# A batched matmul with scale and add: the mid-kernel transfers cut to four tiles, in another order

## The chip, the cores and the metric

The kernel runs on one core of a Trainium2 chip. The metric is the device time of one execution in microseconds. Lower is better.

## The reference

```python
batch, m, k, n = 16, 512, 1024, 768       # all float32
def reference(x, weight, scale, add_value):
    return (scale * np.matmul(x, weight) + add_value).astype(np.float32)
```

The batch and row dimensions flatten to 8192 rows of x (33.6 MB). The weight is 1024 x 768 (3.1 MB), the added tensor and the output are 8192 x 768 (25.2 MB each). Everything together, 87 MB moves between HBM and the chip's working memory.

## The kernel before

The 8192 rows are cut into 64 tiles of 128 rows. The row that a tile puts on partition p is row 64p + t, so several consecutive tiles of one partition lie side by side in HBM, and one transfer can fetch n tiles as 128 rows of n x 4 KB (x) or n x 3 KB (the added tensor and the output).

Two large buffers hold the tiles in rotation: `xs` has 24 slots for x (tile t in slot t modulo 24), `ao` has 24 slots for the added tensor. The result of a tile is written over its slot of `ao`, and the output is stored from there. So a load of the added tensor for tile t can only be issued when the store of tile t - 24 has landed, and a load of x for tile t only when tile t - 24 has been cast.

The work on one tile goes like this.
- Most tiles: GpSimd casts x to bf16 (`cast_to`, L129), TensorE transposes it (L139), ScalarE copies the transposed tile out of the accumulator memory (L145), TensorE multiplies it with the weight in 16 matmuls (`product`, L161), and VectorE scales the sum and adds the `ao` slot (`finish`, L169).
- Nine pairs of tiles (`PAIRS`: 14 and 15, 19 and 20, up to 54 and 55): GpSimd casts both into `vx` (`cast_pair`, L102), VectorE turns them in 32 x 32 blocks into `vt` (`turn_pair`, L113), in four parts over four steps. TensorE doesn't transpose these.
- The first three tiles are handled apart in `head`, interleaved with the arrival of the weight, which is cast on VectorE (L97).

`step` issues one tile: half of its matmuls, then the transposes of the next tile, the cast of the tile after it and, where a pair lies seven tiles ahead, that pair's casts; then the other half, the sum, and a part of a pair's turn. GpSimd executes its casts in this order, so a pair's casts stand ahead of later tiles' casts.

All transfers are issued by the one engine SyncE (SP), on one queue, in the order of the list `STREAM`. Its entries are (kind, first tile, number of tiles): x, weight (w), added tensor (a), output (o), and the left and right part of the last tile's output (l, r). An entry's kind says what SP must wait for: a store waits for the sums of its tiles, a load for free slots. SP works its list in order, so an entry that waits holds up those behind it. The compiled program also uses eight semaphores for transfers in turn, so that the issue of a transfer waits for the landing of the eighth one before it.

The order of the other engines' instructions follows from the same loop over `STREAM`: entries that need results run as many steps as they require.

Of the kernel before, what the change touches and what calls it, by code (L numbers as in the profile page):

```python
# [11 lines left out]
STREAM = [  # L12
    ("x", 0, 1), ("x", 1, 1), ("x", 2, 1), ("w", 0, 1), ("w", 1, 1), ("w", 2, 1),
    ("w", 3, 1), ("w", 4, 1), ("w", 5, 1), ("x", 3, 1), ("w", 6, 1), ("w", 7, 1),
    ("a", 0, 3), ("x", 4, 4), ("a", 3, 1), ("a", 4, 4), ("x", 8, 4), ("x", 12, 4),
    ("a", 8, 8), ("x", 16, 8), ("a", 16, 8), ("x", 24, 8), ("o", 0, 8), ("o", 8, 8),
    ("a", 24, 4), ("x", 32, 4), ("a", 28, 8), ("a", 36, 4), ("x", 36, 8), ("o", 16, 8),
    ("x", 44, 4), ("a", 40, 8), ("x", 48, 4), ("o", 24, 8), ("x", 52, 8), ("a", 48, 4),
    ("o", 32, 8), ("a", 52, 4), ("a", 56, 8), ("x", 60, 4), ("o", 40, 8), ("o", 48, 8),
    ("o", 56, 4), ("o", 60, 2), ("o", 62, 1), ("l", 63, 1), ("r", 63, 1),  # L20
]

X_SLOTS = 24
# [267 lines left out]
```

## Time and profile before

| | us |
|---|---|
| median of 11 runs | 213.59 (211.66 to 215.73) |
| the profiled execution's own time | 213.94 |
| its span, first to last instruction | 212.0 |
| TensorE matmul busy | 194.1 |
| VectorE busy | 131.0 |
| GpSimd busy | 63.5 |
| ScalarE busy | 49.4 |
| transfer queue, share of 16 engines' span | 97.9% |

All numbers below that come from the profile are of that one execution. The profile names engines PE (TensorE), DVE (VectorE), ACT (ScalarE), POOL (GpSimd) and SP (SyncE); "SPq" is SP's own queue of transfer issues. A group or a wait is given by line, engine and operation, written tile and read tile. The forty slices divide the span into stretches of 5.3 us; a digit is the busy share in tenths.

### The profile page before, as it was taken

The numbers are of one execution on the slowest core, as the hardware profiler recorded it, in microseconds if no ns is written. First come the engines' busy times: TensorE is split into PE (matmuls) and PEld (weight loads), VectorE is DVE, ScalarE is ACT, GpSimd is POOL, SyncE is SP. The second block draws the span as 40 slices with busy tenths as digits, with TensorE's granted clock in tenths as the row PEclk, the third lists the DMA queues.
The fourth block names the chain that finished last, engine by engine and source line by source line (L and its number), as shares of the span: only waits on it lengthen the run. The fifth ranks groups of instructions, "written<-read, shape, count | busy, mean of one in ns | idle before, by whom it ended". The sixth has DMA issues, their size and how long they took to land.

```text
span 212.0 us, 3009 instructions
## 1 busy us (share of the span) xinstructions
PE 194.1 (92%) x1195; PEld 118.4 (56%) x1218; DVE 131.0 (62%) x223; ACT 49.4 (23%) x52; POOL 63.5 (30%) x69
## 2 busy tenths in 40 slices
PE   7776399999999999999999899999999999999960
PEld 3443256656666556565656556565656666666630
DVE  1448122319999569859499498986980995322330
ACT  3603123233112113022031031121130310333210
POOL 1310523550080180710900714508007510133000
PEclk9999889999999999999999999999999999999996
DMA  6999999999999999999999999999999999999994
GB/s 239 409 417 444 405 439 414 442 445 420 439 427 456 414 427 422 379 441 433 443 424 428 436 414 439 413 420 425 447 395 429 422 383 413 351 420 434 420 410 176
DMA packets 6781, 87.22 MB, mean 411 GB/s; under 512 B 752, under 2 KB 880, under 8 KB 2928
## 3 DMA queue, kind: packets, MB, share of 16 engines
q1 hardware_dynamic: 6768, 87.03, 97.9%
q8 instruction: 9, 0.15, 0.3%
q14 instruction: 4, 0.03, 0.0%
HBM read 61.87 MB, written 25.17 MB: 410 GB/s over the span
## 4 chain that ended last, share of the span: by engine, by line
DMA 44%; PE 39%; DVE 5%; POOL 4%; issue 3%; SPq 1%; ACT 0%; POOLq 0%; ACTq 0%
DMA xs<-in_x_dram 41%; PE mm L161 35%; PE tp L139 4%; DVE vt L113 3%; DMA ao<-in_weight_dram 3%; POOL xb L129 2%; POOL vx L102 2%; DVE ao L169 2%; SPq L241 1%; ACT xt L145 0%; SPq L93 0%; POOLq L129 0%; POOLq L102 0%; ACTq L145 0%
## 5 line engine op out<-in xcount | busy, mean ns | idle before, releaser
L161 PE MATMUL mm<-w_bf,xt 128*128 128x256 bf16 (+1 forms) x719 | 127.9, 327 | 2.8 <-DVE w_bf L97 1.3
L161 PEld LDWEIGHTS <-xt 128*128 128x128 bf16 x736 | 69.0, 98 | 51.7 <-ACT xt L145 10.8
L169 DVE SCALAR_TENSOR_TENSOR ao<-mm,ao 128x768 f32<-128x768 f32 (+2 forms) x62 | 58.3, 944 | 56.4 <-PE mm L161 42.9
L145 ACT COPY xt<-tp 128x1024 bf16<-128x1024 bf16 (+1 forms) x49 | 46.7, 960 | 150.1 <-PE tp L139 150.1
L113 DVE STREAM_TRANSPOSE vt<-vx 32x256 f32<-32x256 f32 x144 | 62.7, 436 | 6.9 <-POOL vx L102 4.7
L129 POOL CAST xb<-xs 128x1024 bf16<-128x1024 f32 x43 | 43.4, 1040 | 42.7 <-DMA xs<-in_x_dram 30.0
L161 PE MATMUL mm<-w_bf,vt 128*128 128x256 bf16 (+1 forms) x282 | 49.1, 325 | 0.3
L102 POOL CAST vx<-xs 128x1024 bf16<-128x1024 f32 x18 | 18.2, 1040 | 81.7 <-DVE vt L113 44.3
L161 PEld LDWEIGHTS <-vt 128*128 128x128 bf16 x288 | 28.0, 98 | 17.8 <-DVE vt L113 0.3
L139 PE MATMUL tp<-identity,xb 128*128 128x128 f32 x184 | 28.8, 278 | 6.8 <-POOL xb L129 5.7
L139 PEld LDWEIGHTS tp<-identity,xb 128*128 128x128 f32 x184 | 21.5, 142 | 13.8 <-POOL xb L129 6.8
L97 DVE CAST w_bf<-ao 128x768 bf16<-128x768 f32 x8 | 4.5, 560 | 4.8 <-DMA ao<-in_weight_dram 4.8
L87 PE MATMUL warm<-zeros 128*128 128x512 bf16 x10 | 3.7, 546 | 1.2 <-DVE zeros L75 1.2
L125 DVE CAST xb<-xs 128x512 bf16<-128x512 f32 x3 | 1.3, 427 | 4.7 <-DMA xs<-in_x_dram 4.7
L127 POOL CAST xb<-xs 128x512 bf16<-128x512 f32 x2 | 1.7, 866 | 4.6 <-DMA xs<-in_x_dram 4.6
L87 PEld LDWEIGHTS <-zeros 128*128 128x128 bf16 x10 | 1.2, 133 | 3.2 <-issue 1.9
L228 DVE TENSOR_TENSOR ao<-ao 128x768 f32<-128x768 f32 x3 | 2.7, 951 | 0.0
L197 DVE TENSOR_SCALAR ao<-mm 128x768 f32<-128x768 f32 x2 | 1.8, 953 | 1.0 <-PE mm L161 1.0
L127 ACT ACT_TABLE_LOAD x1 | 1.3, 1283 | 0.7 <-PEq L272 0.7
L127 ACT CAST xb<-xs 128x512 bf16<-128x512 f32 x1 | 0.6, 618 | 2.2 <-DMA xs<-in_x_dram 2.2
L194 ACT ACTIVATE ao<-mm 128x768 f32<-128x768 f32 x1 | 0.8, 817 | 0.0
L75 DVE MEMSET zeros<- 128x256 uint32 x1 | 0.3, 272 | 0.9 <-PEq L272 0.9
(6 smaller groups left out, 0.9 us busy)
## 6 DMA issues: line engine op xcount, KB each, us to landing
out_dram<-ao SPq DMA_DIRECT2D x7, 3072.0 KB, 23.9
xs<-in_x_dram SPq DMA_DIRECT2D x4, 4096.0 KB, 33.9
ao<-in_add_value_dram SPq DMA_DIRECT2D x5, 3072.0 KB, 16.1
xs<-in_x_dram SPq DMA_DIRECT2D x7, 2048.0 KB, 17.0
ao<-in_add_value_dram SPq DMA_DIRECT2D x5, 1536.0 KB, 16.5
ao<-in_weight_dram SPq DMA_DIRECT2D x8, 384.0 KB, 7.3
xs<-in_x_dram SPq DMA_DIRECT2D x4, 512.0 KB, 4.6
out_dram<-ao SPq DMA_DIRECT2D x1, 1536.0 KB, 13.1
```

What stands on the lines that cost most here:

```text
L87: nc.tensor.matmul(warm[:, 0:CUT], zeros[:, 0:P], zeros, start=True, stop=True)
L97: nc.vector.tensor_copy(w_bf[:, j + i, :], ao[:, s + i, :])
L102: nc.gpsimd.tensor_copy(vx[:, i, :], xs[:, (t0 + i) % X_SLOTS, :])
L113: nc.vector.transpose(vt[b:b + 32, :, 32 * a:32 * a + 32], pairs[32 * a:32 * a + 32, :, b:b + 32])
L127: other(xb[:, K // 2:K], src[:, K // 2:K])
L129: nc.gpsimd.tensor_copy(xb, src)
L139: nc.tensor.transpose(tp[:, c, :], pairs[:, c * P:(c + 1) * P], identity)
L145: nc.scalar.copy(dst[:, c:c + q, :, :], src[:, c:c + q, :, :])
L161: nc.tensor.matmul(mm_tiles[t, cols[0]][:, n0:n1], lhs(t, j), w_bf[:, j, n0:n1], start=(j == 0), stop=(j == KJ - 1))
L169: nc.vector.scalar_tensor_tensor(a, mm_tiles[t, part][:, n0:n1], float(scale), a, op0=mybir.AluOpType.mult, op1=mybir.AluOpType.add)
L228: nc.vector.tensor_add(ao[:, t, :], ao[:, EARLY_AT + t, :], ao[:, t, :])
L241: nc.sync.dma_start(xs[:, k:k + n, :], x_v[:, s:s + n, :])
```

## The change

The list `STREAM` is replaced. The first twelve entries (four tiles of x and the weight, one tile each) and the last four (two tiles, one tile and two parts of one) stay. In between, every transfer is now four tiles long, apart from the first four tiles of the added tensor, which are loaded as three and one as they were. Before, 16 of the transfers in between were eight tiles long: seven stores, five loads of the added tensor and four loads of x. The list has 63 entries where it had 47. The order differs too: the first store stands behind 20 tiles of x and 12 of the added tensor, where it stood behind 32 and 24. The load of x for tiles 4 to 7 stands behind the load of the added tensor for tile 3, where it stood ahead of it.

```diff
 STREAM = [
     ("x", 0, 1), ("x", 1, 1), ("x", 2, 1), ("w", 0, 1), ("w", 1, 1), ("w", 2, 1),
     ("w", 3, 1), ("w", 4, 1), ("w", 5, 1), ("x", 3, 1), ("w", 6, 1), ("w", 7, 1),
-    ("a", 0, 3), ("x", 4, 4), ("a", 3, 1), ("a", 4, 4), ("x", 8, 4), ("x", 12, 4),
-    ("a", 8, 8), ("x", 16, 8), ("a", 16, 8), ("x", 24, 8), ("o", 0, 8), ("o", 8, 8),
-    ("a", 24, 4), ("x", 32, 4), ("a", 28, 8), ("a", 36, 4), ("x", 36, 8), ("o", 16, 8),
-    ("x", 44, 4), ("a", 40, 8), ("x", 48, 4), ("o", 24, 8), ("x", 52, 8), ("a", 48, 4),
-    ("o", 32, 8), ("a", 52, 4), ("a", 56, 8), ("x", 60, 4), ("o", 40, 8), ("o", 48, 8),
-    ("o", 56, 4), ("o", 60, 2), ("o", 62, 1), ("l", 63, 1), ("r", 63, 1),
+    ("a", 0, 3), ("a", 3, 1), ("x", 4, 4), ("a", 4, 4), ("x", 8, 4), ("a", 8, 4),
+    ("x", 12, 4), ("x", 16, 4), ("o", 0, 4), ("x", 20, 4), ("a", 12, 4), ("x", 24, 4),
+    ("a", 16, 4), ("a", 20, 4), ("o", 4, 4), ("a", 24, 4), ("a", 28, 4), ("x", 28, 4),
+    ("o", 8, 4), ("x", 32, 4), ("a", 32, 4), ("o", 12, 4), ("x", 36, 4), ("x", 40, 4),
+    ("o", 16, 4), ("x", 44, 4), ("a", 36, 4), ("x", 48, 4), ("o", 20, 4), ("a", 40, 4),
+    ("o", 24, 4), ("o", 28, 4), ("a", 44, 4), ("o", 32, 4), ("a", 48, 4), ("x", 52, 4),
+    ("o", 36, 4), ("o", 40, 4), ("a", 52, 4), ("x", 56, 4), ("x", 60, 4), ("a", 56, 4),
+    ("o", 44, 4), ("o", 48, 4), ("a", 60, 4), ("o", 52, 4), ("o", 56, 4), ("o", 60, 2),
+    ("o", 62, 1), ("l", 63, 1), ("r", 63, 1),
 ]
```

The code is otherwise the same, three lines further down.

## The prediction

> **What bounds the kernel now.** I read the totals by engine and the forty slices first, then what SP's issues waited for, then the rate by stretch, and last the chain and the timelines around those places where the matmul waits.
>
> ```profile
> PE 194.1 (92%) x1195; PEld 118.4 (56%) x1218; DVE 131.0 (62%) x223; ACT 49.4 (23%) x52; POOL 63.5 (30%) x69
> PEclk9999889999999999999999999999999999999996
> DMA  6999999999999999999999999999999999999994
> GB/s 239 409 417 444 405 439 414 442 445 420 439 427 456 414 427 422 379 441 433 443 424 428 436 414 439 413 420 425 447 395 429 422 383 413 351 420 434 420 410 176
> q1 hardware_dynamic: 6768, 87.03, 97.9%
> ```
>
> Two resources are full at once: TensorE 92% of the span, the transfer queue 97.9%. The traffic is fixed: 87.03 MB whatever the order. After 5 us no slice of the DMA row is below 9 until the last, so the only ways to change the end are the rate, an empty queue, or a matmul that finishes so late that the last stores find no backlog.
>
> ```profile
> core 0: us, PE busy (x) PEld busy (x) DVE busy (x) ACT busy (x) POOL busy (x), PEclk, DMA share, GB/s
> 5.30:13.00 7.70, 6.46 (x37) 3.68 (x38) 4.06 (x8) 3.22 (x6) 1.73 (x2) 1.00 1.03 409
> 25.00:37.00 12.00, 11.90 (x69) 7.46 (x71) 2.87 (x3) 3.83 (x4) 4.66 (x5) 0.88 1.01 429
> 41.50:71.00 29.50, 29.29 (x188) 18.30 (x191) 23.10 (x42) 8.10 (x8) 8.92 (x9) 1.00 1.00 430
> 80.00:170.00 90.00, 88.36 (x556) 54.49 (x566) 70.70 (x128) 19.23 (x19) 31.95 (x32) 1.00 1.00 425
> 170.00:187.00 17.00, 16.89 (x108) 10.42 (x108) 9.71 (x15) 4.05 (x4) 2.08 (x2) 1.00 0.98 382
> ```
>
> The windows' last column is the rate. Single tiles (3 and 4 KB a row) reach 409 GB/s; four-tile loads at 25 to 37 us 429; eight-tile loads at 41.5 to 71 us 430. So four tiles as such are nearly as fast as eight. Once stores share the queue it is 425, and at 170 to 187 us only 382; another window, 80 to 205 us, answers 419.
>
> ```profile
> SPq L247 <- DMA out_dram<-ao: 97.8, 5, 33.8
> SPq L255 <- DVE ao L169: 60.5, 8, 18.8
> out_dram<-ao SPq DMA_DIRECT2D x7, 3072.0 KB, 23.9
> xs<-in_x_dram SPq DMA_DIRECT2D x4, 4096.0 KB, 33.9
> ao<-in_add_value_dram SPq DMA_DIRECT2D x5, 3072.0 KB, 16.1
> ```
>
> SP waits 97.8 us for a store to free ao slots before an add load (L247), but the queue has tens of us of work by then, so this costs nothing while enough lies ahead of the waiting issue. The x7, x4 and x5 are the sixteen eight-tile transfers.
>
> ```profile
> 39.42 2.02 POOL L102 CAST vx<-xs 128x1024 bf16<-128x1024 f32 x2 [2.77 <-DMA xs<-in_x_dram]
> 41.39 3.01 POOL L129 CAST xb<-xs 128x1024 bf16<-128x1024 f32 x3
> 160.28 2.02 POOL L102 CAST vx<-xs 128x1024 bf16<-128x1024 f32 x2 [11.58 <-DMA xs<-in_x_dram]
> 44.73 0.60 PE L139 MATMUL tp<-identity,xb 128*128 128x128 f32 x4
> 121.05 0.66 PE L139 MATMUL tp<-identity,xb 128*128 128x128 f32 x4 [0.90 <-POOL xb L129]
> 164.64 0.60 PE L139 MATMUL tp<-identity,xb 128*128 128x128 f32 x4
> ```
>
> GpSimd runs in order: a pair's two casts (L102) whose x is late hold up the ordinary casts (L129) that TensorE's next transposes need. TensorE has one such gap in 180 us, 0.90 us at 121. Its end is 205.2 us; the last store is issued at about 205.6, its landing and the closing waits fill the rest of the 212.0 us span. In the trace's landing records the sixteen parts of the last transfer land from 208.6 to 211.15: one DMA engine is some 2.6 us behind the others, and it sets the end. Its backlog hides a later matmul.
>
> **What the Trainium skill says.** DMA: Bandwidth & Descriptors, Bandwidth, gives 78% of peak for a lone 1 MB transfer and 97% for 16 MB. Here the trace disagrees in size, because transfers queue back to back: 1.5 to 2 MB give 429 GB/s. Its part on small descriptors names a fixed overhead per packet; the trace agrees: in the packet records a 12,288 B row takes 460 ns (median), a 24,576 B row 912, a 16,384 B row 611, a 32,768 B row 1213, so 8 ns more for two halves of the add or output rows and 9 ns for x. Its part on the anatomy of one DMA says that waits happen on the issuing sequencer; SP's waits above agree, so a blocked issue holds up all later ones. Its part on completion says that sixteen engines finish independently and only all of them count as landed; the 2.6 us spread is that.
>
> **The change, part by part.** Only SP's list changes; PE, DVE, ACT and POOL instructions keep their kinds, counts and order.
>
> (1) Sixteen more transfers, 47 to 63. Each DMA engine takes 8 of the 128 rows and one 9 ns completion write. Twelve splits of add or output: 12 x (8 x 8 + 9) = 876 ns. Four of x: 4 x (8 x 9 + 9) = 324 ns. Sum 1.20 us on a full queue, nothing beside it: I count it whole. Sixteen more issues on SP (0.33 to 0.43 us each, near 6 us) are free: SP is waiting anyway.
>
> (2) Stores begin earlier and alternate more. Before the first store lie 29.36 MB now and 18.35 MB afterwards, so it moves at about 44 instead of 71 us (11.0 MB at 430). The changes between reads and writes go from 9 to 21. At the mixed rate of 419 against 430 for 27 us: 2.6% of 27 = 0.7 us. Bounds: 0 if alternation isn't what slows it; if the loss scales with the changes, 125 us x 2.6% = 3.2 us becomes 7.5, so +4.3. I take 0.7: in the 80 to 170 us window four of these changes pass at 425.
>
> (3) Waits on ao slots. Before, the add load of tile 56 waits for the store of 32 to 39, with one four-tile load ahead of it (issued at 171.30); that is where 382 GB/s stands. It goes. New is the add load of tile 28, which needs the store of tiles 4 to 7 landed with only the add load of 24 between: 3.7 us of queue against the spread of up to 2 us plus some 2 us from issue to first byte. The faster engines may stand empty for 0 to 0.6 us near 78 us; the slow one, still behind, doesn't. Also at most eight transfers can be unfinished (eight semaphores in turn; the ninth issue waits for the first): eight of 1.6 to 2.1 MB are still 30 us of work, so this costs nothing. I count 0.
>
> (4) TensorE. x of tiles 4 to 7 now goes behind the add load of tile 3: 24.47 - 23.50 = 0.97 us later, and TensorE is waiting for just that (4.8 us idle at 24.7), so all later steps move by 0.97. The x of 12 to 15 goes behind a further add load, 39.37 + 3.7 = 43.1; two pair casts and one plain (3.0) give 46.1 against a transpose wanted at 44.73 + 0.97 = 45.7: with the handover 0.5 us. The x of 52 to 55 has 67.11 MB up to its end, before 66.06: 160.1 + 2.5 + some 0.7 of part 1 + 0.5 of part 2 = 163.8, casts to 167.0, against 164.64 + 0.97 + 0.5 - 0.9 = 165.2: 1.8 us. The 0.90 at 121 goes, as x of 36 to 39 comes 7 us earlier. TensorE ends at 205.2 + 0.97 + 0.5 + 1.8 - 0.9 = 207.6, the last issue at 208.0. The first load, on an empty queue, needs 3.4 us with 1.3 of moving; the last store moves 0.4, so 2.5: 210.5. The queue's end is 211.15 + 1.2 + 0.7 = 213.05, so TensorE's 2.4 us stay hidden, with 2.5 us to spare.
>
> Sum: 213.94 (the profiled execution's own time, 1.9 above its span) + 1.20 + 0.7 = 215.8. That execution lies 0.35 above the median of 213.59 and I make no allowance for it, the eleven runs being spread from 211.66 to 215.73.
>
> **Rivals.**
> - *Only the row overhead* (no loss from mixing): 213.94 + 0 to 1.2, some 215.0. For it: 425 in the 80 to 170 us window. Against: slices of 379, 395, 383, 351, all after stores began.
> - *TensorE or the alternation becomes the bound.* Adds are late too: that of 60 to 63 has 82.31 of 87.03 MB up to its end, which the queue now reaches half-way between landings at 196.6 and 203.8, so 200.2 + 1.9 = 202.1; its first sum is wanted at 196.4 + 2.4 = 198.8. That of 56 to 59 lands where x of 60 does now, 188.8 + 1.9 = 190.7, against 184.1 + 2.4 = 186.5. Three accumulators let TensorE run two tiles (6 us) ahead, so this is covered by 2 us. If mixing costs 3 us rather than 0.7, x of 52 slips 2 us more, the adds 2 to 3, and TensorE ends near 210.5: 213.94 + 1.2 + 3 = 218.1. Against: it needs a rate of 410, seen in single stretches only.
> - *Not slower.* The weak stretch at 170 to 187 us costs (430 - 382)/430 x 17 = 1.9 us, and stems from the one narrow wait of part 3. The new order issues all loads after 150 us well ahead, so if the stretch returns to 430 and nothing replaces it: 213.94 + 1.2 - 1.9 = 213.2. It decides if the gain exceeds 1.2. Against: the same stretch holds slow packets of x of 60, whose issue was not late; and tile 28 has a narrow wait of its own.
>
> **How the numbers follow.** Forecast (215.8, within 1 us) 0.50; overhead alone 0.22; worse 0.16; not slower 0.12. About 1% is what a measurement of this kernel can tell from no change, here 211.5 to 215.7. The forecast lies on that line: 0.33 slower, 0.17 same. With the worse case 0.16 slower; overhead alone all same; not slower: 0.05 same, 0.07 faster. Slower 0.49, same 0.44, faster 0.07. Range: from 213.0 (the gain of 1.9 kept) to 218.4 (3 us and more of mixing).
>
> **What would show it.** In the changed profile: the queue's share still near 98%; the GB/s row uneven from about the ninth slice, no longer from the fourteenth; TensorE idle longer at 25 us, by about 1 us, with waits on L129's counterpart near 46 and 165 us; its end near 207.5; span near 213.9. It is wrong if the DMA row drops in the middle (an empty queue), if TensorE's waits sum to over 4 us, or if 170 to 187 us runs at 430 and the span stays under 212.5.

## The result, and the profile after

The changed kernel takes 215.66 us (median of 12 runs, 214.28 to 217.06); the ratio to the kernel before is 1.011, interval 1.0078 to 1.0141. The ratio leaves out those runs of the kernel before that took over 1.5% longer than its quickest; its median of 213.59 us keeps them. The profiled execution took 214.28 us with a span of 212.5, the quickest of the twelve, so its span hides most of the difference; what it shows well is where the time lies.

The page of the changed kernel, engines first, then the forty slices and the transfer queue:

```profile
PE 195.5 (92%) x1195; PEld 119.3 (56%) x1218; DVE 131.1 (62%) x223; ACT 49.4 (23%) x52; POOL 63.6 (30%) x69
PEclk9999859999999999999999999999999999999999
DMA  6999999999999999999999999999999999999994
GB/s 241 408 417 428 428 433 419 429 425 417 429 426 424 413 407 407 321 436 426 432 429 423 433 428 426 433 418 439 417 436 414 433 429 429 421 437 422 428 385 178
q1 hardware_dynamic: 9072, 87.04, 98.1%
```

The queue is as full as before (98.1%), and its DMA row as even. What differs is the GB/s row. The slices of 383, 413 and 351 near the end are gone, and there is a new low: 321 in the slice from 85.0 to 90.3 us, after 413, 407 and 407. By windows:

```profile
45.00:71.00 26.00, 25.79 (x165) 16.02 (x167) 20.76 (x38) 7.02 (x7) 8.94 (x9) 1.00 1.01 423
71.00:90.00 19.00, 18.89 (x121) 11.68 (x122) 14.24 (x27) 4.05 (x4) 4.98 (x5) 1.00 1.01 387
90.00:170.00 80.00, 77.99 (x491) 48.16 (x500) 62.73 (x113) 16.19 (x16) 29.89 (x30) 1.00 1.01 427
170.00:187.00 17.00, 16.89 (x109) 10.47 (x110) 10.25 (x17) 4.05 (x4) 5.04 (x5) 1.00 1.01 428
```

The same stretches of the kernel before that the prediction doesn't show:

```profile
71.00:90.00 19.00, 18.89 (x119) 11.55 (x120) 14.49 (x27) 3.04 (x3) 8.98 (x10) 1.00 1.00 420
90.00:170.00 80.00, 78.42 (x494) 48.39 (x502) 61.56 (x112) 17.20 (x17) 27.95 (x28) 1.00 1.01 427
```

The last column is the rate. It counts the bytes of a packet where the packet starts, so neighbouring windows can trade a few per cent. 170 to 187 us rose from 382 to 428 GB/s; 71 to 90 us, at 420 before, is at 387. The windows from 90 to 170 us are alike, 427. With 427 as the level, the new low costs 19 x (427 - 387)/427 = 1.8 us in this execution. So the mixed stretch from 90 to 170 us isn't slower than the rest.

SP's waits and its timeline around that place (start, duration, what was issued):

```profile
SPq L250 <- DMA out_dram<-ao: 94.5, 8, 24.2
44.09 0.34 SPq L258 DMA_DIRECT2D out_dram<-ao  x1
51.95 24.87 SPq L250 DMA_DIRECT2D ao<-in_add_value_dram  x2
76.91 0.38 SPq L244 DMA_DIRECT2D xs<-in_x_dram  x1
```

The two add loads are those of tiles 24 and 28. The second waits some 24 us for the store of tiles 4 to 7 to land, and meanwhile SP puts nothing on the queue. When it goes out at 76.5 us, just ahead of x of 28, only the add load of 24 is left in the queue. In the packet records the 16,384 B rows that start between 81 and 90 us, all of them rows of x of 28, take 788 ns on average, up to 2204, against a median of 611 over the run. In the landing records the add load of 28 lands 3.69 us after the transfer ahead of it, as its bytes need at 428 GB/s; x of 28 lands 6.4 us after that, where its bytes need 4.9.

TensorE's four places of interest:

```profile
25.89 1.11 PE L142 MATMUL tp<-identity,xb 128*128 128x128 f32 x4 [5.79 <-POOL xb L132]
47.31 0.60 PE L142 MATMUL tp<-identity,xb 128*128 128x128 f32 x4
122.43 0.60 PE L142 MATMUL tp<-identity,xb 128*128 128x128 f32 x4
167.46 0.66 PE L142 MATMUL tp<-identity,xb 128*128 128x128 f32 x4 [1.30 <-POOL xb L132]
203.85 4.10 PE L164 MATMUL mm<-w_bf,xt 128*128 128x512 bf16 x24
```

The first of them in the kernel before:

```profile
24.74 1.12 PE L139 MATMUL tp<-identity,xb 128*128 128x128 f32 x4 [4.83 <-POOL xb L129]
```

It waits 5.79 instead of 4.83 us at the start, 1.30 near 167 us, no longer at 121, and ends at 208.0 instead of 205.2.

### The profile page after: what moved, and what is told of

Same layout as the page of the kernel before. It is cut to its first block, busy times and chain, and to the rows that moved or that the text cites. A ratio compares the mean times of both kernels' runs of the same rounds, so it can differ in the third digit from the quotient of the medians.

```text
span 212.5 us, 3041 instructions
## 1 busy us (share of the span) xinstructions
PE 195.5 (92%) x1195; PEld 119.3 (56%) x1218; DVE 131.1 (62%) x223; ACT 49.4 (23%) x52; POOL 63.6 (30%) x69
## 3 DMA queue, kind: packets, MB, share of 16 engines
q1 hardware_dynamic: 9072, 87.04, 98.1%
## 4 chain that ended last, share of the span: by engine, by line
DMA 63%; PE 27%; POOL 3%; SPq 2%; issue 2%; DVE 1%; POOLq 0%
DMA out_dram<-ao 38%; PE mm L164 23%; DMA xs<-in_x_dram 22%; PE tp L142 4%; DMA ao<-in_weight_dram 3%; POOL xb L132 2%; POOL vx L105 1%; SPq L244 1%; DVE ao L172 1%; SPq L96 1%; SPq L250 0%; POOLq L132 0%; POOLq L105 0%; SPq L258 0%
## 5 line engine op out<-in xcount | busy, mean ns | idle before, releaser
L164 PE MATMUL mm<-w_bf,xt 128*128 128x256 bf16 (+1 forms) x719 | 129.2, 329 | 3.0 <-DVE w_bf L100 1.3
```

What stands on the lines that cost most here:

```text
L164: nc.tensor.matmul(mm_tiles[t, cols[0]][:, n0:n1], lhs(t, j), w_bf[:, j, n0:n1], start=(j == 0), stop=(j == KJ - 1))
```

## The experiments

All ratios are to the kernel before, measured on the same chip. Q stands for the queue, T for TensorE, N for the narrow wait, M for the mix of stores and loads. A wait is called narrow when the load that waits for a store to land has little queued between that store and itself, so that the queue runs short before the load can be issued.

**Which resource sets the end.** One chunk of the contraction is left out, in both kernels:

```diff
+        if t >= EARLY and j == 3:
+            return
         for n0, n1 in cols:
             nc.tensor.matmul(
```

> The kernel before, with one of the eight chunks of the contraction left out of the product of all tiles from 3 on, which takes about 0.33 us of TensorE from each of 61 tiles, 20 us in all. All transfers and their order stay. Theory Q: at most 1 to 2 us less than before (ratio 0.992 to 1.000), as the queue is full anyway. Theory T: 15 us or more less (ratio under 0.94).

> The changed kernel with the same chunk of the contraction left out. Theory Q: the distance between the two orders stays near 2 us though TensorE has 20 us to spare, ratio to before 1.002 to 1.011 and about 1.01 to the other light kernel. Theory T: both light kernels run alike, well under before.

Measured: 1.0017 (0.999 to 1.0044) and 1.0128 (1.0078 to 1.0178). The busy lines of the two pages:

```profile
PE 181.9 (86%) x1096; PEld 109.0 (51%) x1096; DVE 131.0 (62%) x223; ACT 49.2 (23%) x52; POOL 63.4 (30%) x69
```

```profile
PE 181.9 (85%) x1096; PEld 108.8 (51%) x1096; DVE 130.7 (61%) x223; ACT 49.4 (23%) x52; POOL 63.4 (30%) x69
```

TensorE's busy time fell from 194.1 and 195.5 to 181.9 us (less than the 20 us of work; the mean granted clock was 0.951 and 0.948 in these two executions, 0.984 with the whole product), and the time fell in neither order, nor did the distance between them shrink. The transfer queue sets the end of both kernels; T is out for the changed kernel as it stands.

```diff
-("a", 0, 3), ("a", 3, 1), ("x", 4, 4),
+("a", 0, 3), ("x", 4, 4), ("a", 3, 1),
```

> The changed kernel with x of tiles 4 to 7 put back ahead of the add load of tile 3, one swap. TensorE's second start at 25.9 us should come 1.0 us earlier in every theory. Theory Q: the end doesn't move, ratio to before 1.010 as with the changed kernel. Theory T: the end moves by that 1.0 us, ratio 1.0055.

Measured: 1.0146 (1.0111 to 1.0181). It isn't faster, as Q has it; whether it is slower than 1.011 the intervals don't tell.

**The length of a transfer.** The order of before, each eight-tile entry written as two of four:

```diff
-("a", 8, 8), ("x", 16, 8), ...
+("a", 8, 4), ("a", 12, 4), ("x", 16, 4), ("x", 20, 4), ...
```

> The order of before, with each of its sixteen eight-tile transfers cut into two four-tile ones that follow each other. This isolates the length of a transfer. Theory Q (the transfer queue sets the end; 1.2 us are the fixed cost of sixteen more transfers, some 0.7 us the stores that share the queue earlier): +1.2 us, ratio to before 1.0056, since stores start no earlier. Theory T (TensorE's later finish sets the end, because x arrives later in the new order): the order is that of before, so 1.000. A third, S (four-tile transfers as such are the whole of the loss, also through restarts of the queue and fewer bytes in flight): 1.011.

Measured: 0.9981 (0.9958 to 1.0003). Q's 1.0056 and S's 1.011 lie outside. T's 1.000 lies inside, at the edge, but T was put out by the light kernels, so this agreement says little. The windows of this kernel show why the total isn't the price of the length:

```profile
71.00:90.00 19.00, 19.00 (x121) 11.64 (x120) 14.54 (x26) 3.04 (x3) 9.58 (x10) 1.00 1.01 426
170.00:187.00 17.00, 17.00 (x112) 10.48 (x110) 9.34 (x15) 4.05 (x4) 2.08 (x2) 1.00 1.01 427
```

The low stretch at 170 to 187 us is gone as well: cut in halves, the add load of 56 waits for the store of 32 to 35 alone, and has the store of 36 to 39 and the add load of 52 ahead of it. This suggested theory N, that a store-bound issue with one short transfer ahead of it is what costs time, in both orders.

**The narrow wait.** One swap in each order, and one put in on purpose.

```diff
 # in the changed kernel
-("a", 24, 4), ("a", 28, 4), ("x", 28, 4),
+("a", 24, 4), ("x", 28, 4), ("a", 28, 4),
```

> The changed kernel with one swap: x of tiles 28 to 31 ahead of the add load of 28 to 31, so that two transfers (8.6 us of queue) instead of one (3.7 us) lie ahead of the issue that waits for the store of tiles 4 to 7. Theory N (the narrow wait at 76 us lets the queue run short, and the slow stretch at 76 to 90 us follows from it): the stretch returns to some 425 GB/s and the time falls by 2 to 3 us, ratio to before 0.997 to 1.003. Theory M (stores among the loads from 45 us on are what slows the new order): no change, ratio 1.011.

Measured: 1.0003 (0.9976 to 1.0031). Within the interval the whole difference to the kernel before is gone with one swap. The window of this kernel:

```profile
71.00:90.00 19.00, 19.00 (x123) 11.80 (x122) 14.35 (x26) 4.05 (x4) 7.68 (x8) 1.00 1.01 427
```

```diff
 # in the kernel before
-("a", 52, 4), ("a", 56, 8), ("x", 60, 4),
+("a", 52, 4), ("x", 60, 4), ("a", 56, 8),
```

> The kernel before with one swap: x of tiles 60 to 63 ahead of the add load of 56 to 63, which puts 8.6 instead of 3.7 us of queue ahead of the issue that waits for the store of 32 to 39 at 171 us. Theory N: the slow stretch at 170 to 187 us returns to some 425 GB/s, the time falls by 1.5 to 2 us, ratio 0.991 to 0.993. Theory M: that stretch is slow because of its mix of stores and loads, which stays, so 1.000.

Measured: 0.9948 (0.9927 to 0.997), and when measured again further down 0.9966 (0.994 to 0.9993). It is faster than both kernels. The window went from 382 to

```profile
170.00:187.00 17.00, 16.65 (x108) 10.22 (x107) 9.43 (x15) 3.37 (x4) 3.41 (x4) 1.00 1.02 436
```

The gain, 0.7 to 1.1 us, is less than the 1.5 to 2 expected; 187 to 205 us fell from 425 to 413 in its profile, so part is given back at the end. Between 187 and 208 us the packet records show the sixteen engines empty for 0.7 us on average (1.1 us in the second measurement's profile), where the kernel before has none. That fits a quicker queue that catches up with TensorE's last sums; it wasn't tested.

```diff
 # in the halved order of before
-("o", 4, 4), ("o", 8, 4), ("o", 12, 4), ("a", 24, 4), ("x", 32, 4),
+("o", 4, 4), ("a", 24, 4), ("x", 32, 4), ("o", 8, 4), ("o", 12, 4),
```

> The order of before in halves (ratio 0.998 when measured), with a narrow wait put in on purpose: the add load of tiles 24 to 27, which waits for the store of tiles 0 to 3, goes ahead of the stores of 8 to 15, so that only the store of 4 to 7 (3.7 us) lies ahead of it, and x of 32 to 35 follows it as x of 28 does in the changed kernel. Theory N: 2 to 3 us are lost near 77 to 90 us, ratio 1.007 to 1.012. Theory M: the number of changes between reads and writes goes from 9 to 11 and the stores start no earlier, so under 0.5 us, ratio 0.998 to 1.000.

Measured: 1.0036 (1.0013 to 1.0058), against 0.9981 without it: 0.0055 or 1.2 us, under the 2 to 3 expected. The window has the loss in the right place, 19 x (427 - 397)/427 = 1.3 us:

```profile
71.00:90.00 19.00, 19.00 (x122) 11.66 (x122) 14.44 (x26) 3.04 (x3) 9.57 (x10) 1.00 1.00 397
```

So a narrow wait can be taken out and put in, and time goes and comes with it; M, which expected no change in each of the three, is out as the main cause. The size varies from case to case.

How much queue is enough can be read from the landing records of all fourteen profiles. For each store-bound add load they give how long after its issue the transfer ahead of it landed, and how much later it and the next transfer landed, in sum, than their bytes need at 428 GB/s.

| queue left at the issue | cases | late in sum |
|---|---|---|
| 3.6 us (one four-tile add load or store) | 7 | 1.3 to 2.6 us in each |
| 4.8 to 5.0 us (one four-tile x load) | 10 | 0 to 0.6 us in eight; 0.9 and 1.7 us in two |
| 7 to 10 us | 30 | 0.6 us at most |

The changed kernel has one of the middle kind too, the add load of 32 behind x of 32, which the prediction didn't name. In its own profile that one landed in time. The two late ones are this same load, in the light changed kernel and in the one with x of 4 to 7 put back.

```diff
 # in the changed kernel
-("a", 28, 4), ("x", 28, 4), ("o", 8, 4),
+("a", 28, 4), ("o", 8, 4), ("x", 28, 4),
```

> The changed kernel with one swap: the store of tiles 8 to 11 ahead of x of 28 to 31, behind the add load of 28. The narrow wait stays; what follows it first is a store instead of an x load. The traces show the slow packets not in the add load alone, but in the x load after it. Theory N1 (the short queue costs what the empty engines lose, and an x load that comes next is slow of itself because all engines restart together): the loss shrinks to 0.5 to 1 us, ratio 1.002 to 1.006. Theory N2 (the restart slows whatever comes next): 1.011 stays.

Measured: 1.0218 (1.0165 to 1.0272), worse than either theory. The low stretch stays, and TensorE meets a late x for it:

```profile
71.00:90.00 19.00, 19.00 (x123) 11.69 (x122) 14.23 (x27) 4.05 (x4) 4.99 (x5) 1.00 1.00 391
```

```profile
97.45 1.11 PE L142 MATMUL tp<-identity,xb 128*128 128x128 f32 x4 [3.70 <-POOL xb L132]
```

391 with a store next, 387 with an x load next: N1, that it is the x load which is slow, falls. In the landing records it is now the add load of 28 that comes 1.9 us late, and the rows of x of 28 take 618 ns on average. The 3.7 us at 97 us come from x of 28 standing one store later. TensorE's last sum is so late that the last store was issued at 213.6 us and landed 1.8 us later: here TensorE binds, and the DMA share from 187 to 205 us is only 0.90. This is the cover that the changed kernel had left, used up.

**The length alone.** Both without a narrow wait, on one chip:

> The order of before with x of 60 to 63 ahead of the add load of 56 to 63, everything in halves of four tiles. Neither this kernel nor its eight-tile counterpart below has a store-bound issue with only one four-tile transfer ahead of it, so their difference is the length of the transfers alone. Theory Q (each of sixteen more transfers costs its 64 to 81 ns of packets and completions on a full queue): 1.2 us more than the counterpart, a ratio of 1.0056 between the two, and some 1.000 to before. Theory F (the fixed cost disappears in the queue's own slack): the two agree within 0.3 us.

> The eight-tile counterpart of the run above, measured beside it on the same chip: the kernel before with x of 60 to 63 ahead of the add load of 56 to 63. Ratio to before 0.995 as when it was measured first.

Measured: 0.997 (0.9949 to 0.9991) and 0.9966 (0.994 to 0.9993); medians 212.21 and 211.94. The difference is 0.1 us by the ratios and 0.3 by the medians. The ratio between the two is 1.0004, give or take 0.0034 (the two half-widths, squared, added, and the root), so the 1.0056 of Q lies outside, and up to some 0.8 us isn't excluded. The rate of the halves and of their eight-tile counterpart from 90 to 170 us:

```profile
90.00:170.00 80.00, 79.29 (x501) 49.30 (x510) 63.74 (x116) 17.08 (x17) 28.27 (x29) 1.00 1.01 427
90.00:170.00 80.00, 79.31 (x501) 49.20 (x510) 63.03 (x114) 17.20 (x17) 28.03 (x29) 1.00 1.01 427
```

The pair isn't as clean as the expectation has it. The eight-tile kernel has a load with only one four-tile transfer ahead of it, the add load of 40 behind x of 44 (4.8 us).

The landing records of the seven kernels in the order of before, four with eight-tile transfers and three in halves, show two things that work against each other. From 40 to 73 us, where only loads move, an eight-tile add load lands 7.29 to 7.31 us after the transfer ahead of it and two halves 7.36 to 7.40; for x it is 9.70 to 9.72 against 9.75 to 9.82, one 9.81 of the eight-tile kernels aside. By the medians that is 0.06 to 0.09 us for each load cut in two, near the 0.073 and 0.081 of the prediction; the stores show 0 to 0.06 in most places. By an estimate from these, sixteen cuts cost some 0.9 us.

On the other side x of 48, x of 52 to 59 and the add load of 48 land 0.4 to 1.5 us late in sum in the four eight-tile kernels, and at most 0.1 in the three with halves. By these records the fixed cost is there, and what F calls the queue's slack is a loss elsewhere in the long order that hides it; each kernel has one profile, so it is read from them and not tested.

**What is left in the new order.** Both swaps in the changed kernel, then the same without the one chunk of the contraction:

> The changed kernel with both swaps: x of 28 ahead of the add load of 28, and x of 4 to 7 ahead of the add load of tile 3. With the narrow wait gone, the last store of the kernel with the first swap alone was issued at 207.1 us and landed from 208.7 to 209.9, so little backlog is left behind TensorE. Theory T' (once the queue no longer loses time, TensorE's later start binds): 0.5 to 1 us less than with the first swap alone, ratio to before 0.996 to 0.998. Theory Q: the slow engine's queue still sets the end, ratio 1.000.

Measured: 1.0007 (0.998 to 1.0033), so x of 4 to 7 alone changes nothing here either; TensorE gets its 1.0 us at 25 us and waits 1.08 and 0.59 us at 46 and 166 us instead.

> The changed kernel with both swaps (ratio to before 1.0007), and with one of the eight chunks of the contraction left out from tile 3 on, so that TensorE has 20 us to spare. What is asked is the rest of 0.8 us between that order and the halved order of before (0.997), both without a narrow wait. Theory M' (stores share the queue from 45 us on): the queue carries it, so 1.000 stays. Theory T' (TensorE starts later or waits for x in the new order): it falls to 0.997. A difference of this size is near what five rounds can tell.

Measured: 0.9964 (0.9939 to 0.9989), the level of the halved order of before. The two intervals overlap a little (0.998 to 0.9989), so it leans to TensorE for the last 0.8 us, and against the mix of stores and loads; I don't call it shown. The halved order of before wasn't run with the lighter product, and it might have fallen too.

## Why the prediction was right, and where it wasn't

The forecast of 215.8 against 215.66 is right in sign and size. Its bound is right too: the queue sets the end and TensorE's delay stays under it. But the sum of 1.20 + 0.7 isn't how the time came about; that it comes to the measured 2.1 us (2.3 by the ratio) is luck.

- Part 1, the 1.20 us of sixteen more transfers: the cost of a cut is about right for the loads (0.06 to 0.09 us in the landing records) and smaller for the stores, some 0.9 us in all by the estimate above. The step that failed is "nothing beside it: I count it whole": the long transfers were taken to run without loss, and they lose 0.4 to 1.5 us between 138 and 165 us; why is not shown. The net, measured as time, is 0.1 to 0.3 us.
- Part 2, the 0.7 us of earlier stores: its cause isn't borne out. With 21 changes between reads and writes in all, some 12 of them between 90 and 170 us, this stretch runs at 427 GB/s, as it does with 9 and 5. I had taken a rate for the whole of 80 to 205 us, with the low stretch in it, as the price of mixing. Two readings were off as well: six changes, not four, pass in the window at 425, and the first store follows a load that landed at 48.1 us, so 44 was too early (11.0 MB at 430 GB/s are 25.6 us).
- Part 3, the waits on ao slots, "I count 0": this is the step on which the answer hung. The narrow wait was named, with its place and its time (near 78 us), and priced by the emptiness of the faster engines, 0 to 0.6 us. Worked out from the packet records, the emptiness, averaged over the sixteen engines, is 0.04 us in the changed kernel and up to 0.7 us in the six others with a narrow wait. What was left out are the packets after it, which were slow: in these seven, what packets take above the median of their size comes to 1.3 to 2.1 us per engine in the low stretch, and to 0.2 at most in the same stretches of the seven kernels without one. The narrow wait cost 1.0110 - 1.0003, or 2.3 us. On the other side the old narrow wait went, which I left to a rival at 1.9 us and which is worth 0.7 to 1.1. The new one less the old one is 1.2 to 1.6 us; with 0.8 for what is left in the order and 0.1 to 0.3 for the length, 2.1 to 2.7. This sum has to close, as the kernels form a chain from one order to the other; it isn't a check.
- Part 4, TensorE: right. The first delay was 0.96 us (0.97 said), the wait at 121 us went, that of x of 52 to 55 was 1.30 (1.8 said), the end 208.0 (207.6 said). The wait for x of 12 to 15 (0.5 said) didn't appear in this execution: TensorE's clock was lower at 25 to 37 us (0.72 against 0.88) and it came later itself. In the kernel with both swaps, which waits 1.0 us less at 25 us, it did (1.08 us). That all this stays hidden is shown by the two light kernels; that it ends soon by the store ahead of x of 28.
- The 2.6 us between landings: the sixteen parts of the last transfer don't have one engine far behind the others. Eleven land from 208.6 to 209.4 us and the last five at 210.1, 210.4, 210.7, 210.75 and 211.15. The last is 2.6 us behind the first and 0.4 behind the next.
- The rivals: "not slower" had the right mechanism for its half, the old stretch did return to 428, and named what would undo it. The worse case needed the mix to be slow, which it isn't.
- The signs: the queue's share and TensorE's end came as said. The span was 212.5 and not near 213.9, and the GB/s row wasn't uneven from the ninth slice on. The last sign of being wrong, 170 to 187 us at 430 with a span under 212.5, was all but met, with 428 and 212.5. It was drawn for a case in which nothing takes the old stretch's place, and was read on the quickest of twelve executions.

## What to carry to other kernels

Where a full queue sets the end, look at the issues that wait for an earlier transfer's landing and count how much is queued between the two. Here 3.6 us of queue lost time in all seven profiles, 4.8 us in some, and 7 to 10 us at most 0.6 us. Swap a load that is already free to go ahead of the waiting one; it took one line in each order and was worth 0.3 to 0.5% in the order of before and 1.1% in the new one. And before a low rate is put down to a kind of traffic, see whether it is spread over that traffic or sits in one place behind one wait.

## What the runs showed of the hardware that I hadn't expected

- After a narrow wait most of the loss isn't in empty engines (0.04 to 0.7 us of emptiness against 1.3 to 2.1 us of slow packets). The slow packets come in the transfer behind the wait, the one after it, or both: mostly x of 28 in the changed kernel. Why they are slow is open; a store in place of the x load didn't help (391 against 387 GB/s).
- Transfers of 1.5 and 2 MB did nearly as well as those of 3 and 4 MB on a queue kept full: 427 GB/s for both from 90 to 170 us, and 0.1 to 0.3 us of difference in the whole time. Each row's packet takes 8 to 9 ns more per two halves, and this does show in the landings of loads that nothing disturbs, 0.06 to 0.09 us for each load cut in two. The table of the Trainium skill that the prediction quotes (DMA: Bandwidth & Descriptors, Bandwidth) was measured on transfers issued from GpSimd, so its figures and these, of a queue that SyncE keeps full, aren't of the same thing.
